# A hybrid decoder layer on one core: where the first gate/up block lies, which PSUM bank a gate product takes, and the order of the first head's query chain

## The chip, the cores and the metric

The kernel runs on one core of one Trainium2 chip. The metric is the device time of one execution in microseconds (us); the figure for a kernel is the median of its timed runs. A separate execution is taken by the hardware profiler, and every time inside the kernel below is counted from that execution's first instruction.

The engines are named as in the profile: PE (TensorE matmuls), PEld (TensorE weight loads, which overlap PE), DVE (VectorE), ACT (ScalarE), POOL (GpSimd) and SP (SyncE, which here only issues transfers). SBUF is the working memory, PSUM the memory into which PE writes, in banks of 128 x 512 float32.

## The reference, cut to what matters

One decoder layer over 16 learned meta tokens and 512 tokens, width 2048, float32:

```python
h = concatenate([meta, x])
n = rmsnorm(h, g_mix)
q, k, v, gb, gc, u = split(n @ w_in)              # 8 heads x 128, and 1024 convolution channels
q, k = rmsnorm per head(q, g_q), rmsnorm per head(k, g_k)
o_attn = stick_breaking_attention(q, k, v)        # strictly causal, log space, reverse cumulative sum
o_conv = gb * causal_dwconv3(gc * u, conv_w)
o = concatenate([rmsnorm(o_attn, g_attn_out), rmsnorm(o_conv, g_conv_out)])
h = h + o @ w_out
n2 = rmsnorm(h, g_ffn)
h = h + (silu(n2 @ w_gate) * (n2 @ w_up)) @ w_down
return h[16:]
```

A row of the attention is `w = exp(log_beta + log_pass)` with `log_pass` the sum of `log(1 - beta)` over the later keys.

## The kernel before, in words

**Arithmetic.** Everything lies transposed, channels on partitions and tokens along the free axis. A float32 value is kept as two float32r parts: `hi` (an ACT cast) and `lo` (a DVE subtraction of `hi` from the value). A product is then three matmuls, hi x hi, hi x lo and lo x hi. `split` (L349) does this for activations, `split_quad` (L196) for a piece of weights: the ACT cast is L203, the DVE subtraction L206. Three such pieces fit into `sw_split`, so the cast of a piece waits until PE has read the piece three places earlier. `prepare` (L235) makes the next piece and issues the load of a later one from SP (`load_wide`, L177, `load_quad`, L168). A piece of kind "wide" is 1024 rows of one 128-column tile.

**Stages.** First come the eight heads (`head`, L551). For head 0 the products of k, q and v run interleaved while x is loaded (L448 to L459); for head h >= 1 they run one after another (`pk`, `pq`, `pv`), and the small steps of earlier heads are threaded between their matmuls: `after(n, work)` (L316) sets work to be written down n ticks later, and `tick` counts one k tile of a product. So the k product of head 1 carries ticks 1 to 16 after head 0's own products, its q product ticks 17 to 32. The order on each engine is then made by a list scheduler, which goes by priority and by its own estimate of when each instruction is ready; `tc.high_priority` raises the priority, `tc.issue_after(i)` puts what follows behind instruction i where it is on the same engine, and `tc.keep_in_program_order` fixes the place as written. No engine changes that order at run time.

`qk_norm` (L525) gives the normalised k or q: the squares are split (`sh`, `sl`), `finish` sums them over partitions on PE (`ss_...`, L537), adds eps on DVE (L539), and calls `rsqrt` (L352), which is ACT Ln, Exp and Square (L356 to L358) and DVE steps L360, L361 and L362, the last of which writes the result; then `split` casts it (ACT L350) and makes the low part (DVE L350). `attend` (L586) turns v with PE transposes (L590) and splits it, then computes the logits `z` in three blocks of keys, b = 2, 1, 0 (L605 to L610), the log terms on ACT (L631 to L633) and DVE (L634, L635), the causal masks on POOL (L622). `sums` (L653) adds up over later keys on PE into `c` (L658 to L664), and `mix` (L688) multiplies with v. Small PSUM tiles (`small`, L66) come from the pool `sm` of four banks in rotation; `pp` holds two buffers of two banks each for products of 528 or 512 columns.

After the heads come the first convolution channels: `pc0`, `pu0` and the gate products `pb0` (L762) and `pb1` (L824), each read out by one DVE multiplication (L765, L826). Then `sm` and `pp` are released and `xyz` (two buffers each of one bank, y, z and x) takes their place.

**Strassen-like pairs.** All later products but the output projection run as pairs: `pair_product` (L875) makes seven blocks of matmuls (`block_product`, L846: L862, L865, L866) into the banks y, x and z, in place of eight. For gate/up the seven activation blocks `acts[0]` to `acts[6]` are eight tiles of 128 x 256 each, hi and lo. The first pair uses them in the order 5, 0, 1, 2, 3, 4, 6; the later ones in the order 0, 1, 2, 3, 4, 5, 6. There are 44 gate/up pairs.

**Around the output projection.** `oapool` holds `oa_last` (attention's outputs of heads 4 to 7) and `oc_hi`; `ocpool` holds the low parts of the convolution's outputs. Output tile i is the product over `oa` (all attention heads), then over `oc`. The blocks f5, f0 to f3 are made on chip, column by column, as the tiles end. The blocks f4 and f6 find no room and are written to DRAM (`fx`, L1130) column by column, from POOL. Once tile 15's products are written down (i = KT - 2), `oapool`, `ocpool` and `mpool` are released, and f4 and f6 are given places on that memory (L1067 to L1069). Then `load_f(4, 7)` (L1071) loads f4 in two transfers, hi and lo, of seven columns; the eighth is made on chip (`fifth_block`). `load_f(6, 8)` (L1133) loads f6 likewise with eight columns, after the last store to `fx`. A tile laid over released memory waits for those that used the tiles under it.

Counted from the start of the left part of `mpool`, in bytes per partition, and worked out from the shapes in the code: `mpool` 0 to 16704, `ocpool` to 33280, `oa_last` 33280 to 49664, `oc_hi` 49664 to 66048. Before the change f4 lies at 15712 to 32352 and f6 at 32352 to 48992.

Of the kernel before, what the change touches and what calls it, by code (L numbers as in the profile page):

```python
# [33 lines left out]
def hybrid_layer(ctx: ExitStack, tc: tile.TileContext, xT, w_in, w_out, w_gu, w_down, vecs, out):  # L34
# [118 lines left out]
    READ_FIRST = (*range(CONV + 9, CONV + 13), *range(CONV + FT, SIX))  # L153
    latest, opened, cast, put_off = [None], [None], [None], []

# [79 lines left out]
    def prepare():  # L235
        kind, i, s = pieces[len(split_w)]
        with tc.high_priority():
# [7 lines left out]
            if kind == "wide":  # L245
                split_quad(wide[i, s], 8)
                load_wide(i, s + 4)
                return
# [103 lines left out]
    def rsqrt(dst, v, n, y=None, t=None, eng=ve, times=None):  # L352
# [8 lines left out]
        eng.scalar_tensor_tensor(t[:, :n], t[:, :n], -0.5, v, ALU.mult, ALU.mult)  # L361
        eng.scalar_tensor_tensor(dst, t[:, :n], 1.5, y[:, :n], ALU.add, ALU.mult)  # L362
        return last

# [160 lines left out]
    def qk_norm(read, dst, parts_of, name, at=("sh", "sl")):  # L525
# [7 lines left out]
        def finish():  # L533
            v = t512(L, "v", 2)[:, :cols]
            for a, b in cuts:
# [5 lines left out]
                )  # L541
            rsqrt(dst, v, cols, times=raw)
            hi, lo, n = parts_of
            split(hi, lo, dst[:, :n])

        return finish

    selected = [None]
    SEG = [(0, 512), (512, 912), (912, 1344)]

    def head(h):  # L551

        if h:
            pk = pp.tile([P, 2, 512], F32, tag="pp", name=f"pk{h}")
            product(parts_of_all(pk), n_hl)
        read = read_qk(flat(pk), g_k, L) if h else read_k0
        kn = kns[0]
# [24 lines left out]
        else:  # L582
            after(2, scale_v)
        after(6 if h else 15, lambda: attend(h, kn, kh, kl, qn, qh, ql, vts[0]))

    def attend(h, kn, kh, kl, qn, qh, ql, vt):  # L586

# [8 lines left out]
        ve.tensor_copy(v32[:, :P], ta[:, 384:512])  # L596
        ve.tensor_copy(v32[:16, P:], tb[:16, :P])


        zs = {}  # L600
# [106 lines left out]

        after(14, lambda: sums(2))

# [51 lines left out]
    conv3(y0, cu0, 0)  # L761
    pb = pp.tile([P, 2, 512], F32, tag="pp", name="pb0")  # L762
    product([(pb[:, 0, :], META, L)], n_hl)
    gb0 = t512(L, "v", 2)[:, :SEQ]
    ve.tensor_tensor(gb0, pb[:, 0, :], r[:, META:], ALU.mult)  # L765
    assert not waiting
# [57 lines left out]
    pb = pp.tile([P, 2, 512], F32, tag="pp", name="pb1")  # L824
    product([(pb[:, 1, :], META, L)], n_hl)
    ve.tensor_tensor(gb1, pb[:, 1, :], r[:, META:], ALU.mult)  # L826
    sm.release()
# [128 lines left out]
    for j in range(1, HEADS):  # L956
        conv_pair(j, scale_a if j == 1 else None)
        if j == 1:
            gated(ocf[1], 1, ocf[1], gb1, gb1)
        elif j == 2:  # L960
            scale_a_rest()
        elif j % 2:
            gate_pair(j)
    mixp.release()
    oapool = open_pool("oapool")
# [4 lines left out]
    oa_last = oapool.tile([P, 4, 2, SEQ], F32R, name="oa_last")  # L970
    oa_at += [oa_last[:, h] for h in range(4)]
    for h in range(HEADS):
        gp.dma_start(oa_at[h], oa_dram[h])
# [24 lines left out]
    def pad(pool, n):  # L998
        pool.tile([P, n // 4], F32, name=f"pad_{pool.name}")

# [35 lines left out]
    for i, j in enumerate(OUT_TILES):  # L1036
# [6 lines left out]
        if i == KT - 2:  # L1043
# [115 lines left out]
    def h_scale_rest():  # L1159
        with tc.issue_after(opened[0].ins):  # L1160
            last = waiting_h.pop()()
        with tc.issue_after(last.ins):
            sc.preload_act_table_set("silu_and_others")
# [214 lines left out]
```

## Time and profile before

| | |
|---|---|
| timed runs | 2032.9, 2033.38 and 2033.34 us; median 2033.34 us |
| the profiled execution | 2035.46 us; its span from the first to the last instruction 2033.8 us |
| mean granted TensorE clock | 0.999 of full speed |
| PE busy | 2023.1 us, 99% of the span |
| DVE busy | 1725.6 us, 85% |
| ACT busy | 1078.3 us, 53% |

The profile page gives the busy time of each engine, the span in 40 slices and the costliest groups of instructions. The view of the waits lists for one engine what it waited for. The timeline gives the instructions of an engine in order: start, duration, engine, line, operation, output and inputs, shape, and in brackets the idle time before it with what released it. The windows give for a stretch of time the busy time of each engine, the granted PE clock, the share of the DMA engines in use and their rate. A matmul's recorded duration overlaps with the next one's, since they are pipelined: a matmul of 512 columns starts about 0.23 us after the one before it, one of 256 columns about 0.11 us.

### The profile page before, as it was taken

The page shows a single profiled execution, that of the slowest core. Times are in us where ns is not written, and L with a number is a line of the kernel's source. Part 1 is how long each engine was busy: PE and PEld are TensorE (multiplying, and loading weights), DVE is VectorE, ACT ScalarE, POOL GpSimd, SP SyncE. Part 2 cuts the span into 40 slices and gives each one's busy share as a digit, 9 for nine tenths or more (in the row PEclk, how much of TensorE's full clock was granted, in tenths as well). Part 3 has the DMA queues.
Part 4 walks back from the last instruction along what each step waited for, and adds up shares of the span by engine and source line. Part 5 has one row for each costly group of instructions (what it writes and reads, how often), then busy time and mean ns, then how long its engine had stood idle before and what let it go on. Part 6 is the DMA issues. An engine that isn't in the chain of part 4 may idle for free.

```text
span 2033.8 us, 39697 instructions
## 1 busy us (share of the span) xinstructions
PE 2023.1 (99%) x16158; PEld 1963.8 (97%) x16158; DVE 1725.6 (85%) x2199; ACT 1078.3 (53%) x1559; POOL 339.4 (17%) x507
## 2 busy tenths in 40 slices
PE   9999999999999999999999999999999999999999
PEld 9899999899998889999999999999999999999999
DVE  7777777698887878999998988988988978888888
ACT  7776666444454444555555555555555554444443
POOL 0111111200014440112111111111111243131211
PEclk9999999999999999999999999999999999999999
DMA  6243344833365555557555555555555999797864
GB/s 221 94 146 125 116 144 127 281 104 106 103 207 171 171 160 193 151 151 208 150 166 162 143 175 161 143 174 161 145 172 161 278 342 350 171 315 200 222 146 93
DMA packets 156664, 356.31 MB, mean 175 GB/s; under 512 B 13696, under 2 KB 68224, under 8 KB 155712
## 3 DMA queue, kind: packets, MB, share of 16 engines
q1 hardware_dynamic: 72784, 216.76, 33.7%
q0 software_dynamic: 83696, 136.99, 25.4%
q8 instruction: 127, 2.08, 0.4%
q14 instruction: 57, 0.47, 0.1%
HBM read 275.78 MB, written 77.92 MB: 174 GB/s over the span
## 4 chain that ended last, share of the span: by engine, by line
PE 96%; DVE 1%; ACT 1%; DMA 1%; issue 0%; POOL 0%; SPq 0%; ACTq 0%; POOLq 0%; DVEq 0%
PE x L862 13%; PE x L865 13%; PE x L866 13%; PE z L862 7%; PE z L865 7%; PE z L866 7%; PE y L862 3%; PE y L865 3%; PE y L866 3%; PE pv L339 3%; PE pk L339 3%; PE pq L339 2%; PE pv L337 1%; PE pk L337 1%; PE pq L337 1%; DMA f<-fx 1%
## 5 line engine op out<-in xcount | busy, mean ns | idle before, releaser
L203 ACT CAST sw_split<-sw_in 128x1024 fp32r<-128x1024 f32 (+3 forms) x671 | 662.5, 989 | 707.3 <-PE x L865 173.4
L206 DVE TENSOR_TENSOR sw_split<-sw_in,sw_split 128x1024 fp32r<-128x1024 f32 (+3 forms) x671 | 776.7, 1158 | 145.4 <-ACT sw_split L203 137.9
L865 PE MATMUL x<-f,sw_split 128*128 128x256 f32 x1408 | 388.1, 276 | 2.2 <-DMA f<-fx 2.2
L862 PE MATMUL x<-f,sw_split 128*128 128x256 f32 x1408 | 388.2, 276 | 0.2 <-ACT sides L887 0.2
L866 PE MATMUL x<-f,sw_split 128*128 128x256 f32 x1408 | 387.9, 276 | 0.0
L865 PEld LDWEIGHTS x<-f,sw_split 128*128 128x128 f32 x1408 | 265.1, 188 | 2.4 <-DMA f<-fx 2.4
L862 PEld LDWEIGHTS x<-f,sw_split 128*128 128x128 f32 x1408 | 265.0, 188 | 1.1 <-ACT sides L887 0.6
L866 PEld LDWEIGHTS x<-f,sw_split 128*128 128x128 f32 x1408 | 265.0, 188 | 0.0
L1179 POOL DMA_DIRECT2D fd<-s x147 | 103.7, 922 | 711.0 <-DVE s L350 635.4
L862 PE MATMUL z<-f,sw_split 128*128 128x256 f32 x704 | 193.6, 275 | 0.0
L865 PE MATMUL z<-f,sw_split 128*128 128x256 f32 x704 | 193.6, 275 | 0.0
L866 PE MATMUL z<-f,sw_split 128*128 128x256 f32 x704 | 193.6, 275 | 0.0
L216 DVE TENSOR_TENSOR sw_in<-sw_in 128x1024 f32<-128x1024 f32 (+1 forms) x164 | 187.7, 1145 | 6.1 <-DMA sw_in<-w_in 1.2
L862 PE MATMUL x<-ring,sw_split 128*128 128x256 f32 x608 | 167.2, 275 | 0.0
L865 PE MATMUL x<-ring,sw_split 128*128 128x256 f32 x608 | 167.2, 275 | 0.0
L866 PE MATMUL x<-ring,sw_split 128*128 128x256 f32 x608 | 167.2, 275 | 0.0
L862 PEld LDWEIGHTS z<-f,sw_split 128*128 128x128 f32 x704 | 132.2, 188 | 0.0
L865 PEld LDWEIGHTS z<-f,sw_split 128*128 128x128 f32 x704 | 132.2, 188 | 0.0
L866 PEld LDWEIGHTS z<-f,sw_split 128*128 128x128 f32 x704 | 132.1, 188 | 0.0
L862 PEld LDWEIGHTS x<-ring,sw_split 128*128 128x128 f32 x608 | 114.1, 188 | 0.0
L866 PEld LDWEIGHTS x<-ring,sw_split 128*128 128x128 f32 x608 | 114.1, 188 | 0.0
L865 PEld LDWEIGHTS x<-ring,sw_split 128*128 128x128 f32 x608 | 114.1, 188 | 0.0
(698 smaller groups left out, 5280.7 us busy)
## 6 DMA issues: line engine op xcount, KB each, us to landing
sw_in<-w_gu SPq DMA_DIRECT2D x176, 512.0 KB, 4.1
sw_in<-w_in SPq DMA_DIRECT2D x90, 512.0 KB, 3.5
fd<-s POOLq DMA_DIRECT2D x147, 256.0 KB, 5.2
sw_in<-w_down SPq DMA_DIRECT2D x96, 384.0 KB, 4.3
ring<-fd POOLq DMA_DIRECT2D x42, 768.0 KB, 17.6
sw_in<-w_out SPq DMA_DIRECT2D x32, 512.0 KB, 3.5
out_T<-d POOLq DMA_DIRECT2D x54, 256.0 KB, 4.8
mix_dram<-st_x POOLq DMA_DIRECT2D x16, 516.0 KB, 4.1
```

The lines of the kernel that those rows point to most:

```text
L203: cast[0] = sc.copy(hi, src)
L206: latest[0] = ve.tensor_tensor(lo, src, hi.bitcast(F32), ALU.subtract)
L216: return ve.tensor_tensor(sums[name], a, b, ALU.add)
L337: pe.matmul(ps, wh, ah[:, a:b], start=k + i == 0, stop=False)
L339: pe.matmul(ps, w, x[:, a:b], start=False, stop=k + i == last and x is (al if used[0] <= n_first else ah))
L862: opening = pe.matmul(p, hi[:, kk], ah, start=start and j == k == 0, stop=False, skip_group_check=skip)
L865: pe.matmul(p, hi[:, kk], al, start=False, stop=False, skip_group_check=skip)
L866: pe.matmul(p, lo[:, kk], ah, start=False, stop=k == n - 1, skip_group_check=skip)
L1179: gp.dma_start(fd[c][s][:, :, k], t[:, :, i])
```

## The change

It has three parts.

1. **f4 and f6 change places.** f6 is laid first, at 15712 to 32352; a pad of 1024 bytes follows, and f4 goes to 33376 to 49776, without the 60 spare elements at its end (`slots` has a parameter for them). A pad of 128 bytes behind `oa_last` moves `oc_hi` to 49792. So f4 now lies over `oa_last` and that pad alone, and f6 over `ocpool` and the end of `mpool`. The order in which they are loaded stays: f4, then f6.
2. **`pb0` goes to a small bank** (the pool `sm`) in place of a buffer of `pp`. The next tile, `pb1`, so takes the other of `pp`'s two buffers, and its first bank in place of the second.
3. **The first head's query chain.** The split of head 0's k (cast and subtraction) is put off until the Square (L358) of its q chain has been issued on ACT. The DVE low part of a "wide" piece of weights, the second one prepared after that, is issued behind the DVE low part of q. Head 1's reads of its k product (L435, L436) are issued behind the ACT cast of head 0's q. The turning of v (`turned`) stays at tick 15, and the logits are written down at tick 21 in place of 15; `sums(2)` follows 9 ticks later in place of 14, at tick 30 in place of 29. `rsqrt` returns its last instruction too, for the bookkeeping.

```diff
-    latest, opened, cast, put_off = [None], [None], [None], []
+    latest, opened, cast, put_off, behind = [None], [None], [None], [], []
...
             if kind == "wide":
-                split_quad(wide[i, s], 8)
+                low = split_quad(wide[i, s], 8, later=True)
+                first = behind.pop(0) if behind else None
+                with tc.issue_after(first.ins) if first else nullcontext():
+                    low()
                 load_wide(i, s + 4)
...
-            rsqrt(dst, v, cols, times=raw)
+            last, _ = rsqrt(dst, v, cols, times=raw)
             hi, lo, n = parts_of
-            split(hi, lo, dst[:, :n])
+            if name == "k0":
+                split_k0.append(lambda: split(hi, lo, dst[:, :n]))
+                return
+            if name != "q0":
+                split(hi, lo, dst[:, :n])
+                return
+            with tc.issue_after(last.ins):
+                split_k0.pop()()
+            split_q0.extend(split(hi, lo, dst[:, :n]))
+            behind.extend([None, split_q0[1]])
...
-        read = read_qk(flat(pk), g_k, L) if h else read_k0
+        with tc.issue_after(split_q0[0].ins) if h == 1 else nullcontext():
+            read = read_qk(flat(pk), g_k, L) if h else read_k0
...
-        after(6 if h else 15, lambda: attend(h, kn, kh, kl, qn, qh, ql, vts[0]))
-
-    def attend(h, kn, kh, kl, qn, qh, ql, vt):
+        if h:
+            after(6, lambda: attend(h, kn, kh, kl, qn, qh, ql, turned(h, vts[0])))
+        else:
+            after(15, lambda: vts.append(turned(h, vts[0])))
+            after(21, lambda: attend(h, kn, kh, kl, qn, qh, ql, vts[1]))
+
+    def turned(h, vt):
...
-        after(14, lambda: sums(2))
+        after(14 if h else 9, lambda: sums(2))
...
-    pb = pp.tile([P, 2, 512], F32, tag="pp", name="pb0")
-    product([(pb[:, 0, :], META, L)], n_hl)
+    pb = small("pb0")
+    product([(pb, META, L)], n_hl)
...
-    product([(pb[:, 1, :], META, L)], n_hl)
-    ve.tensor_tensor(gb1, pb[:, 1, :], r[:, META:], ALU.mult)
+    product([(pb[:, 0, :], META, L)], n_hl)
+    ve.tensor_tensor(gb1, pb[:, 0, :], r[:, META:], ALU.mult)
...
+    pad(oapool, 128)
...
-    def slots(pool, dt, m, n, name, **kw):
+    def slots(pool, dt, m, n, name, tail=60, **kw):
...
-        t = pool.tile([P, c + 64], dt, name=name, **kw)
+        t = pool.tile([P, 4 + c + tail], dt, name=name, **kw)
...
-            for s in (4, 6):
-                acts[s] = slot(fpool_last, F32R, 8, f"f{s}", f"f{s}")
+            acts[6] = slot(fpool_last, F32R, 8, "f6", "f6")
+            pad(fpool_last, 1024)
+            acts[4] = slots(fpool_last, F32R, 1, 8, "f4", tail=0)[0]
```

More of the change, by code (lines that the diff above doesn't have):

```diff
@@ L361, in rsqrt @@
         eng.scalar_tensor_tensor(t[:, :n], t[:, :n], -0.5, v, ALU.mult, ALU.mult)
-        eng.scalar_tensor_tensor(dst, t[:, :n], 1.5, y[:, :n], ALU.add, ALU.mult)
-        return last
+        return last, eng.scalar_tensor_tensor(dst, t[:, :n], 1.5, y[:, :n], ALU.add, ALU.mult)
     def square_sum(acc, src, first, s=None, eng=gp):
@@ L541, in finish @@
                 )
-            rsqrt(dst, v, cols, times=raw)
+            last, _ = rsqrt(dst, v, cols, times=raw)
             hi, lo, n = parts_of
-            split(hi, lo, dst[:, :n])
+            if name == "k0":
[8 more added lines that the diff above has]
+            behind.extend([None, split_q0[1]])
         return finish
+    split_k0, split_q0 = [], []
     selected = [None]
@@ L597, in attend @@
         ve.tensor_copy(v32[:16, P:], tb[:16, :P])
+        return vh, vl, v32
+    def attend(h, kn, kh, kl, qn, qh, ql, v):
+        vh, vl, v32 = v
         zs = {}
@@ L761, in hybrid_layer @@
     conv3(y0, cu0, 0)
-    pb = pp.tile([P, 2, 512], F32, tag="pp", name="pb0")
-    product([(pb[:, 0, :], META, L)], n_hl)
+    pb = small("pb0")
+    product([(pb, META, L)], n_hl)
     gb0 = t512(L, "v", 2)[:, :SEQ]
-    ve.tensor_tensor(gb0, pb[:, 0, :], r[:, META:], ALU.mult)
+    ve.tensor_tensor(gb0, pb, r[:, META:], ALU.mult)
     assert not waiting
@@ L963, in hybrid_layer, with pad @@
             gate_pair(j)
+    def pad(pool, n):
+        pool.tile([P, n // 4], F32, name=f"pad_{pool.name}")
     mixp.release()
@@ L996, in slot @@
         return slots(pool, dt, 1, n, name, tag=tag)[0]
-    def pad(pool, n):
-        pool.tile([P, n // 4], F32, name=f"pad_{pool.name}")
     acts = {}
@@ L1160, in h_scale_rest @@
         with tc.issue_after(opened[0].ins):
-            last = waiting_h.pop()()
+            last, _ = waiting_h.pop()()
         with tc.issue_after(last.ins):
```

## The prediction, made before the changed kernel was run

> **What bounds the kernel now.** The page first, then the view of PE's waits.
>
> ```profile
> span 2033.8 us, 39697 instructions
> ...
> PE 2023.1 (99%) x16158; PEld 1963.8 (97%) x16158; DVE 1725.6 (85%) x2199; ACT 1078.3 (53%) x1559; POOL 339.4 (17%) x507
> ```
>
> ```profile
> PE x L865 <- DMA f<-fx: 2.2, 1, 2.2
> PE warm L84 <- DVE one L80: 1.1, 1, 1.1
> ```
>
> PE is the bound, and the change takes away no matmul. What it can win is PE's idle time: the span less the busy time is 10.7 us, and the longest wait is for f, the second is the kernel's start. Only four waits stand where the change acts: this one, and those of z, y and c, whose rows follow below with their idle time in brackets.
>
> The f wait costs more than its 2.2 us. The windows for PE alone set the undisturbed block before it against the block that waits, both of 24 matmuls; the last number but two is the granted clock:
>
> ```profile
> 781.22:783.94 2.72, 2.72 (x26) 1.00 1.08 414
> 784.61:791.45 6.84, 4.67 (x24) 0.75 0.30 102
> ```
>
> ```profile
> 784.62 0.38 PE L862 MATMUL x<-f,sw_split 128*128 128x256 f32 x1
> 787.16 0.58 PE L865 MATMUL x<-f,sw_split 128*128 128x256 f32 x1 [2.16 <-DMA f<-fx]
> ```
>
> 6.84 - 2.72 = 4.12 us: the second matmul comes 2.54 us after the first in place of 0.11, which is 2.43, and the other 1.7 follow it. The windows of all engines tell why:
>
> ```profile
> 788.00:789.00 1.00, 1.00 (x6) 1.00 (x6) 0.98 (x1) 0.00 (x0) 0.00 (x0) 0.50 0.70 250
> ```
>
> Ahead of the DMA share stands the clock: it is halved, and the mean of 0.75 over 6.84 us makes that half clock 3.4 us long. Half of it, 1.7 us, is lost.
>
> **Part 1, f4 and f6.** The block is the seventh of the first pair, the one that reads f6; f4 had landed. The timeline of POOL shows the issues:
>
> ```profile
> 757.23 0.71 POOL L1130 DMA_DIRECT2D fx<-w  x1 [0.92 <-DVE w L350]
> ...
> 761.69 1.29 POOL L371 TENSOR_TENSOR acc_h<-acc_h,sw_in 128x512 f32<-128x512 f32 x1 [0.61 <-ACT sw_in L370]
> 763.90 0.70 POOL L1130 DMA_DIRECT2D fx<-w  x1 [0.92 <-DVE w L350]
> 767.91 2.87 POOL L1019 DMA_DIRECT2D f<-fx  x4 [3.32 <-PE po15z L842]
> ```
>
> ```profile
> DMA to landing us min/median/max: 7.9/11.4/17.1
> ```
>
> ```profile
> fx<-w POOLq DMA_DIRECT2D x15, 256.0 KB, 2.7
> ```
>
> All four loads of f (the view of that tile on POOL has their times to landing) go out from 767.91, 0.72 us apart (2.87 / 4), released by the last product over the convolution's outputs. The last, issued at about 770.0, lands 17.1 us later, at 787.1, which is when PE goes on. The rates say what it waits for:
>
> ```profile
> 760.00:765.00 5.00, 5.00 (x36) 4.69 (x35) 4.26 (x6) 3.16 (x6) 2.77 (x4) 1.00 0.14 52
> 765.00:770.00 5.00, 5.00 (x44) 5.00 (x43) 3.88 (x8) 2.29 (x5) 2.09 (x3) 1.00 0.67 174
> 770.00:775.00 5.00, 5.00 (x47) 5.00 (x46) 4.46 (x7) 3.77 (x8) 0.78 (x2) 1.00 1.03 327
> ```
>
> From 770 the DMA engines are full; before 765 they idle at a share of 0.14. After the change f4 waits for attention's outputs alone, and PE is done with those here:
>
> ```profile
> 761.59 0.39 PE L842 MATMUL po15x<-oa_last,sw_split 128*128 128x512 f32 x1
> 761.81 0.28 PE L840 MATMUL po15y<-oc_hi,sw_split 128*128 128x256 f32 x1
> ...
> 767.56 0.28 PE L862 MATMUL y<-f,sw_split 128*128 128x256 f32 x1
> ```
>
> So f4's place is free at 762.0 and not at 767.7. Its seventh column was stored at 757.23, and a store lands in 2.7 us (the median of the 15 stores to `fx` above), so that is no limit. POOL is in L371 until 763.0; I put the issue there, 4.9 us earlier. f6 still waits for 767.7 and for its own last column, stored at 763.90. f4's two issues of 0.72 us now stand in POOL's queue ahead of that store or behind it, so it is late by 0 to 1.4 us; nobody but f6 waits for it. Were f4's issue put ahead of L371, POOL would stand for 0.3 us until 762.0, with that sum and the store behind it. SP's loads of weights meet f4's traffic from 763 to 770; at shares of 0.14 and 0.67 there is room, and a piece that landed late would hold PE for as much.
>
> f4's two transfers carry 1.8 MB (128 partitions x 7 x 256 x 4 bytes, twice) and f6's 2.1 MB, worked out from the code. The last of the four landed at 787.1; with f4's share begun 4.9 us earlier on idle engines f6 lands at 787.1 - 4.9 = 782.2. The other bound is a store that queues behind all of f4: the median of 11.4 us parts f4's landings from f6's, so f4 would land by 763.0 + 11.4 = 774.4; then come the store, 2.7, and f6's own stretch, 787.1 - (767.9 + 11.4) = 7.8: 784.9. It is needed at 784.7. I take no wait: 4.1 us won, and the half clock with it. By 0.3 at most the wait is given back: without it the next pair comes 4.1 us earlier upon DVE, whose queue is not paced by PE there:
>
> ```profile
> 791.92 1.05 ACT L203 CAST sw_split<-sw_in 128x1024 fp32r<-128x1024 f32 x1
> ```
>
> ```profile
> 789.28 1.23 DVE L275 TENSOR_TENSOR sw_in<-sw_in 128x1024 f32<-128x1024 f32 x1
> 790.43 1.22 DVE L216 TENSOR_TENSOR sw_in<-sw_in 128x1024 f32<-128x1024 f32 x1
> ```
>
> The third block of that pair would begin at 784.62 + 3 x 2.72 = 792.8. Its weights are what L275 makes; they are cast after it, from 790.5 in 1.05 us, and the low part is a DVE step as large as L216's, 1.22 us from 791.65: 792.9. That is at the limit, so I count 0.2. **Part 1: -3.9 us**, between 0 (f6 as late as now) and -4.1.
>
> **Part 2, the small bank.** The wait view names an ACT cast for y; the timelines of PE and DVE show another releaser, 0.15 us ahead:
>
> ```profile
> 388.30 0.61 PE L339 MATMUL pb<-n,sw_split 128*128 128x512 f32 x2
> 389.79 0.36 PE L862 MATMUL y<-n,sw_split 128*128 128x258 f32 x1 [0.87 <-ACT sw_split L203]
> ```
>
> ```profile
> 388.95 0.69 DVE L826 TENSOR_TENSOR gb<-pb,r 128x512 f32<-128x512 f32 x1 [3.35 <-PE pb L339]
> ```
>
> DVE reads `pb1` out until 389.64, while y's weights may be cast as soon as `pb0`'s are used, before `pb1` begins. y's bank lies on that buffer of `pp`: the pool hands out its two buffers in turn, and by the count of allocations `pb1` is in the first one, on which the first bank of `xyz` falls. With `pb0` gone from `pp`, `pb1` is in the second, below z. z comes two blocks after y, some 5.4 us, when L826 is long over. The last matmul starts at 388.52, y could at 388.75: **1.0 us won**, between 0 (if it were the cast) and 1.04. `pb0`'s new bank served head 7's logits, which are read before that head's sums, and it is read out a whole product (16 k tiles of three matmuls, 16 x 0.68 = 10.9 us) before x takes that bank: nothing; a reader still at work would cost up to its 0.69 us.
>
> **Part 3, the query chain.** Timelines of ACT, DVE and PE:
>
> ```profile
> 55.17 0.51 ACT L350 CAST host<-kn 128x384 fp32r<-128x384 f32 x1 [0.95 <-DVE kn L362]
> 55.59 0.63 ACT L358 ACTIVATE tmp<-tmp 128x512 f32<-128x512 f32 x1
> ...
> 59.44 0.62 ACT L350 CAST host<-tmp 128x512 fp32r<-128x512 f32 x1 [0.28 <-DVE tmp L362]
> ```
>
> ```profile
> 57.59 1.20 DVE L206 TENSOR_TENSOR sw_split<-sw_in,sw_split 128x1024 fp32r<-128x1024 f32 x1
> 58.73 0.67 DVE L362 SCALAR_TENSOR_TENSOR tmp<-tmp,tmp 128x512 f32<-128x512 f32 x1
> ```
>
> ```profile
> 58.67 0.39 PE L337 MATMUL pq<-n,sw_split 128*128 128x512 f32 x1
> 60.11 0.80 PE L605 MATMUL z<-host,host 128*128 128x272 f32 x3 [1.05 <-ACT host L350]
> ```
>
> The first logits wait for the cast of q (59.44 to 60.06), and that chain is held up twice: its Square stands on ACT behind the cast of k, idle for 0.95 us first, and a weight piece's low part of 1.20 us stands on DVE ahead of its last step. Both go. Then the Square starts 0.95 us sooner or more, L362 by another 1.1, and the cast of q ends by about 58.1 (it may meet a weight cast on ACT). PE reaches z at 58.67 + 0.23 = 58.9; tick 21 is five k tiles, 15 matmuls, into the q product, and z stood behind the 16th: the same place. So 60.11 - 58.9 = **1.2 us won**, between 0 and 1.2. What moves behind I cost at nothing: the key casts are needed at the same z; head 1's two reads of `pk` come later by one cast, 0.62 us, and feed head 1's logits, which come after its v product; the weight piece is for that v product, more than ten k tiles of q (7 us) away, and behind it waits one SP load, of a piece four places on, with loads after it that wait for later pieces anyway. Without that cover the piece would cost up to its 1.20 us.
>
> Then the sums over later keys:
>
> ```profile
> 68.31 0.39 PE L339 MATMUL pq<-n,sw_split 128*128 128x512 f32 x1
> 69.20 0.43 PE L658 MATMUL c<-sph,later_r 128*128 128x432 f32 x1 [0.50 <-ACT lw L633]
> ```
>
> 0.66 us lost. The whole chain shifts with z, but PE also arrives 1.2 us sooner; only the later tick (0.68 us at most) and the moved weight step help. Between 0 and 0.66, I take **0.3**.
>
> **The sum** is 3.9 + 1.0 + 1.2 + 0.3 = 6.4 us. The profiled execution took 2035.46 us (span 2033.8); 2035.46 - 6.4 = 2029.1, or 0.31% less. The median, 2.1 us below the profiled one, becomes 2033.34 - 6.4 = **2026.9 us**.
>
> The Trainium skill speaks of the halved clock ("TensorE: Matmul & The Clock Gate", "What's actually happening"): the clock halves after at least one idle window of some 3.4 us, which runs freely. The half-clock stretch agrees in length; the idle time, 2.2 us, is shorter than the page's window. By the free-running window the loss would depend on the phase of an execution, which is the first rival.
>
> **Rivals.**
>
> - *The half clock isn't in the timed runs.* The three differ by 0.5 us, and the profiled one is 2.1 us longer, which leaves room for 1.7. Then part 1 is worth 2.4 - 0.2 and the time is 2028.6. For: that difference. Against: nothing ties it to this place. 0.13.
> - *f6 stays the late one, or f4 isn't issued earlier.* The store of f6's last column would land behind all of f4, or POOL would keep f4's issue behind it. For: the last landing may be tight, 784.9 against 784.7. Against: the idle DMA engines. In full, part 1 is 0 and the time 2030.8; with half the wait and no half clock about 2028.5. 0.16, three quarters of it near 2030.8.
> - *Another wait at head 0.* The scheduler orders all engines anew, and the logits or sums find some other step late: 1.5 us less, 2028.4. 0.07.
> - *f4's new place reads slowly*, the rival on the other side. The 48 matmuls of 256 columns from 761.81 to 767.56 take 0.120 us each on `oc_hi`, the 24 on f 2.72 / 24 = 0.113. Read at 0.120, f4's 44 x 24 matmuls cost 1056 x 0.0067 = 7.1 us, more than the 6.4 won: 2034.0; f6, which moves too, as much again: 2041.1. It decides from 6 ns a matmul on. Against: that block of 2.72 us reads f4 at its old place; f6 moves to just that place, by 16640 bytes, f4 by 17664, both multiples of 256. 0.06, half of it for each size.
>
> The forecast keeps 0.53; 0.05 is for an order elsewhere that I can't see. **Chances.** A measurement of this kernel can tell some 0.2%, 4.1 us, from no change, so faster means below 2029.3: 0.53 and 0.13, 0.04 of the second rival and 0.06 of the third, 0.76. Slower: 0.03 of the slow place and 0.03 of the unseen, 0.06. Same: 0.18. The forecast's own range is 2026.1 to 2028. The wide one reaches from 2025.9 (all four waits gone, 7.0, and a crumb) to 2030.8 (part 1 worth nothing).
>
> **What would show it.** Right: f4's issues near 763 and no wait for f in PE's waits; a granted clock of 1.00 from 780 to 795; y directly after `pb1`; z directly after `pq`, with the Square ahead of the key cast. Wrong: L1019 still at 768, or f6 landing past 785; a y that waits for another bank; a new wait at c; f blocks that take more than 2.72 us in every pair.

## The result, and the profile after

The median of 16 runs fell from 2033.12 to 2029.41 us: a ratio of 0.9981, 95% interval 0.9973 to 0.9989. That is 3.7 us where 6.4 were forecast. The time lies in the prediction's wide range (2025.9 to 2030.8) and outside its own narrow one (2026.1 to 2028), 2.5 us above the forecast. The fall is just short of the 4.1 us that the prediction had set as its bound for "faster", to which it gave 0.76; to no change it gave 0.18.

The two profiled executions differ by more: 2035.46 and 2029.19 us, 6.3 us apart, nearly the forecast's sum. Most of this document is about why these two differences are not the same.

The page of the changed kernel, and its view of PE's waits:

```profile
span 2027.5 us, 39699 instructions
...
PE 2020.7 (100%) x16158; PEld 1961.9 (97%) x16158; DVE 1725.5 (85%) x2199; ACT 1078.1 (53%) x1559; POOL 336.6 (17%) x507
```

```profile
PE warm L84 <- DVE one L80: 1.1, 1, 1.1
PE pk L340 <- ACT n L412: 1.0, 2, 0.7
PE z L627 <- DVE host L353: 0.3, 1, 0.3
PE x L883 <- ACT sides L908: 0.2, 1, 0.2
```

The waits for f, y and c are gone; that of z has shrunk from 1.1 to 0.3 and changed its releaser. The wait of pk, at the kernel's start, differs between traces from nothing to 1.8 us and isn't part of the change. (In the changed kernel L337 has become L340, L339 L342, L350 L353, L357 L360, L358 L361, L362 L365, L605 L626, L862 L883, L865 L886, L1019 L1041.)

**f.** POOL's timeline, and the last line of the view of `f` on POOL:

```profile
759.30 1.29 POOL L373 TENSOR_TENSOR acc_h<-acc_h,sw_in 128x512 f32<-128x512 f32 x1 [0.71 <-ACT sw_in L372]
761.51 0.70 POOL L1153 DMA_DIRECT2D fx<-w  x1 [0.92 <-DVE w L353]
762.10 1.56 POOL L1041 DMA_DIRECT2D f<-fx  x2
766.42 1.42 POOL L1041 DMA_DIRECT2D f<-fx  x2 [2.75 <-DMA fx<-w]
```

```profile
DMA to landing us min/median/max: 6.3/9.7/12.1
```

f4 is issued at 762.1, behind the last store, and f6 at 766.4 and 767.1, once that store has landed. The last one lands at the latest 767.1 + 12.1 = 779.2 us, and PE wants it at 782.5. (PE's timeline runs 2.3 us earlier here than in the profile of before: this block began at 784.62 there and begins at 782.28 now.) The windows around that place:

```profile
774.00:782.20 8.20, 8.20 (x71) 7.79 (x69) 7.67 (x14) 4.16 (x7) 0.00 (x0) 1.00 0.93 343
782.25:785.00 2.75, 2.72 (x23) 2.72 (x24) 2.25 (x2) 0.39 (x1) 0.00 (x0) 1.00 0.01 3
```

In this stretch PE is busy for 2.72 of 2.75 us, the clock is 1.00, and the DMA engines have nothing left to do (share 0.01). By the starts of its matmuls the block that waited takes 2.88 us, since its first one takes 0.23 in place of 0.11, with a wait or without. So what it lost in the profile of before is 6.83 - 2.88 = 4.0 us and not the 4.1 that the prediction had from the block ahead of it.

**y** starts right behind `pb1`, and **c** right behind `pq` (PE's timeline):

```profile
386.14 0.62 PE L342 MATMUL pb<-n,sw_split 128*128 128x512 f32 x2
386.60 0.28 PE L883 MATMUL y<-n,sw_split 128*128 128x258 f32 x1
```

```profile
68.08 0.61 PE L342 MATMUL pq<-n,sw_split 128*128 128x512 f32 x2
68.53 0.36 PE L679 MATMUL c<-sph,later_r 128*128 128x432 f32 x1
```

**z** still loses time. PE and ACT:

```profile
58.34 0.61 PE L342 MATMUL pq<-n,sw_split 128*128 128x512 f32 x2
59.09 0.39 PE L626 MATMUL z<-host,host 128*128 128x272 f32 x1
59.82 0.39 PE L627 MATMUL z<-host,host 128*128 128x272 f32 x1 [0.33 <-DVE host L353]
```

```profile
55.35 0.63 ACT L361 ACTIVATE tmp<-tmp 128x512 f32<-128x512 f32 x1 [1.01 <-DVE kn L365]
55.89 0.50 ACT L353 CAST host<-kn 128x384 fp32r<-128x384 f32 x1
...
58.42 0.62 ACT L353 CAST host<-tmp 128x512 fp32r<-128x512 f32 x1 [0.70 <-DVE tmp L365]
```

z could start 2 x 0.227 after 58.34, at 58.79, and comes 0.30 later; its second matmul comes 0.73 after the first in place of 0.13, another 0.60. The Square (L361) now stands ahead of the key cast, but it still idles 1.01 us for the last step of k.

To split the whole difference I took each matmul's start less that of the one before it, less the usual value for its size, from the two traces. The f block gives 4.0 us, y 1.04, the stretch of head 0 from 50 to 100 us 2.24 (z 0.3, c 0.7, and 1.2 in small gaps, most of them at the matmuls of the sums), and an x block of the convolution at 428 us, 0.39. That makes 7.7. The output projection takes back 1.4: its matmuls start 229 ns apart in place of 227. What is left, 6.3, agrees with the two spans.

### The profile page after: what moved, and what is told of

The parts are those of the page before. It is cut to its first block, busy times and chain, and to the rows that moved or that the text cites. A ratio compares the mean times of both kernels' runs of the same rounds, so it can differ in the third digit from the quotient of the medians.

```text
span 2027.5 us, 39699 instructions
## 1 busy us (share of the span) xinstructions
PE 2020.7 (100%) x16158; PEld 1961.9 (97%) x16158; DVE 1725.5 (85%) x2199; ACT 1078.1 (53%) x1559; POOL 336.6 (17%) x507
## 4 chain that ended last, share of the span: by engine, by line
PE 95%; DVE 2%; ACT 1%; issue 1%; DMA 1%; SPq 0%; POOL 0%; ACTq 0%; DVEq 0%
PE x L883 13%; PE x L886 13%; PE x L887 13%; PE z L886 7%; PE z L883 7%; PE z L887 7%; PE y L886 3%; PE y L887 3%; PE y L883 3%; PE pv L342 3%; PE pk L342 3%; PE pq L342 3%; PE pv L340 2%; PE pk L340 1%; PE pq L340 1%; PE pb L342 1%
## 5 line engine op out<-in xcount | busy, mean ns | idle before, releaser
L883 PE MATMUL x<-f,sw_split 128*128 128x256 f32 x1408 | 387.6, 275 | 0.3 <-ACT sides L908 0.2
L886 PE MATMUL x<-f,sw_split 128*128 128x256 f32 x1408 | 387.3, 275 | 0.0
L883 PEld LDWEIGHTS x<-f,sw_split 128*128 128x128 f32 x1408 | 264.3, 188 | 1.1 <-ACT sides L908 0.6
L886 PEld LDWEIGHTS x<-f,sw_split 128*128 128x128 f32 x1408 | 264.3, 188 | 0.0
L883 PE MATMUL z<-f,sw_split 128*128 128x256 f32 x704 | 193.6, 275 | 0.0
L886 PE MATMUL z<-f,sw_split 128*128 128x256 f32 x704 | 193.6, 275 | 0.0
L883 PE MATMUL x<-ring,sw_split 128*128 128x256 f32 x608 | 167.2, 275 | 0.0
L886 PE MATMUL x<-ring,sw_split 128*128 128x256 f32 x608 | 167.2, 275 | 0.0
L886 PEld LDWEIGHTS z<-f,sw_split 128*128 128x128 f32 x704 | 132.1, 188 | 0.0
L883 PEld LDWEIGHTS z<-f,sw_split 128*128 128x128 f32 x704 | 132.1, 188 | 0.0
L883 PEld LDWEIGHTS x<-ring,sw_split 128*128 128x128 f32 x608 | 114.1, 188 | 0.0
L886 PEld LDWEIGHTS x<-ring,sw_split 128*128 128x128 f32 x608 | 114.1, 188 | 0.0
```

Of the source, the lines that this page charges most:

```text
L883: opening = pe.matmul(p, hi[:, kk], ah, start=start and j == k == 0, stop=False, skip_group_check=skip)
L886: pe.matmul(p, hi[:, kk], al, start=False, stop=False, skip_group_check=skip)
```

## The experiments

Each experiment was timed beside the kernel before on the same chip. "Lowest" is the lowest run of each; where a landing varies it tells more than the median.

| kernel | median, us (runs) | lowest | before beside it: median, lowest | ratio and 95% interval |
|---|---|---|---|---|
| before again | 2031.84 (11) | 2031.48 | 2032.01, 2031.15 | 0.9999 (0.9990 to 1.0007) |
| part 1 alone | 2032.86 (11) | 2032.46 | 2032.01, 2031.15 | 1.0002 (0.9993 to 1.0011) |
| parts 2 and 3 | 2028.36 (11) | 2027.38 | 2032.01, 2031.15 | 0.9983 (0.9975 to 0.9992) |
| changed, pad of 256 | 2027.75 (11) | 2027.23 | 2032.01, 2031.15 | 0.9977 (0.9968 to 0.9986) |
| the same, Square freed | 2026.90 (7) | 2026.70 | 2032.18, 2031.31 | 0.9972 (0.9961 to 0.9983) |
| part 2 alone | 2031.11 (11) | 2030.51 | 2032.18, 2031.31 | 0.9995 (0.9986 to 1.0004) |
| ticks alone | 2032.16 (11) | 2031.23 | 2032.18, 2031.31 | 1.0002 (0.9994 to 1.0011) |
| part 1 alone, pad of 256 | 2031.60 (11) | 2031.28 | 2032.67, 2031.56 | 0.9992 (0.9983 to 1.0001) |
| part 3 alone | 2029.62 (11) | 2028.65 | 2032.67, 2031.56 | 0.9986 (0.9977 to 0.9995) |
| order alone | 2030.36 (11) | 2029.13 | 2032.67, 2031.56 | 0.9986 (0.9977 to 0.9995) |
| Square freed alone | 2029.65 (11) | 2029.05 | 2032.67, 2031.56 | 0.9986 (0.9977 to 0.9995) |

Medians of different rows come from different sittings; they are compared through the column of before.

### The kernel before, once more

No edit.

> The kernel before, unchanged, to see its executions one by one. Two theories of the 2 us by which its profiled execution (2035.46 us) lies above its median (2033.1), and of why the medians part by 3.7 us where the two profiled executions part by 6.3. Varying landing: when f6 lands differs from execution to execution, and with it the wait for f (2.2 us) and the half clock (1.7 us); then the spans scatter over some 4 us, the long ones have a mean clock of 0.999 and the short ones 1.000, and a profile of a short execution shows no wait or a small one for f. Fixed wait: the wait for f stands in every execution, and the scatter comes from elsewhere (the start, the end, work on PE throughout); then clock and span are not tied, and another profile shows the same 4.1 us at this block.

Varying landing, plainly. This profile has no wait for f at all; its three longest waits are

```profile
PE warm L84 <- DVE one L80: 1.1, 1, 1.1
PE z L605 <- ACT host L350: 1.1, 1, 1.1
PE y L862 <- ACT sw_split L203: 0.9, 1, 0.9
```

and f's landing line, which had a median of 11.4 and a maximum of 17.1, reads

```profile
DMA to landing us min/median/max: 5.7/9.1/14.1
```

Over 100 runs of this kernel (33, 23 and 33 beside the other experiments, and these 11), the median is 2032.1 us. In 15 the mean granted clock is 0.999, and these take 2034.82 us or more; in the other 85 it is 1.000, and none takes over 2034.26. 31 of the 100 lie above 2033. The profile that the prediction was made from, 2035.46 us at a clock of 0.999, is such a one.

The windows of both kernels show what is late. Of the profiled execution of before, the last 1.8 us before f6 lands; of this one, the last 1.4:

```profile
784.90:785.90 1.00, 0.11 (x1) 0.00 (x0) 1.00 (x2) 0.00 (x0) 0.00 (x0) 1.00 0.16 61
785.90:786.70 0.80, 0.00 (x0) 0.00 (x0) 0.80 (x1) 0.00 (x0) 0.00 (x0) 1.00 0.11 41
```

```profile
783.40:783.80 0.40, 0.40 (x6) 0.40 (x5) 0.40 (x2) 0.00 (x0) 0.00 (x0) 1.00 1.02 410
783.90:784.90 1.00, 0.95 (x7) 0.51 (x6) 0.69 (x3) 0.00 (x0) 0.00 (x0) 1.00 0.84 332
```

In the late one a share of 0.11 to 0.16 of the 16 engines works, about two of them, while PE stands idle; in the other the transfer ends with all at work. The late execution's last 12 packets of f end one every 0.16 to 0.33 us from 783.2 to 786.6, while in this one the last 12 end within 1.05 us. So f6 isn't late because its traffic is too much; by the share, one or two DMA engines still have a tail to move when the others are done. Why they fall behind is open.

### Part 1 alone, and the output projection

```diff
+    pad(oapool, 128)
...
-            for s in (4, 6):
-                acts[s] = slot(fpool_last, F32R, 8, f"f{s}", f"f{s}")
+            acts[6] = slot(fpool_last, F32R, 8, "f6", "f6")
+            pad(fpool_last, 1024)
+            acts[4] = slots(fpool_last, F32R, 1, 8, "f4", tail=0)[0]
```

> Part 1 alone on the kernel before: the places of f4 and f6 and the pads, PE's order unchanged. By the prediction -3.9 us against a profiled execution that has the full wait and the half clock. By the theory that the landing varies and that the 128-byte pad under oc_hi costs 1.3 us in the output projection: the wait for f gone in the profile, the matmuls on oc_hi and oa at 230 ns in place of 227, and the median of the timed runs only 1 to 2.5 us below before. If the pad has no part in the slower output projection, those matmuls stay at 227 ns here.

The part that the prediction valued at 3.9 us gives nothing in the median, and the 1 to 2.5 us expected here didn't come either: the median is 0.85 us above that of before. Its lowest run is 1.3 us above the lowest of before, and its highest, 2033.38, is 2.2 us below the highest of before, 2035.57. It narrows the runs to 0.9 us and puts them all higher. The windows of 100 us in the output projection, of before again, part 1 alone, the changed kernel and the changed kernel with a pad of 256 bytes, count PE's matmuls in the bracket behind its busy time:

```profile
610.00:710.00 100.00, 100.00 (x443) 82.84 (x442) 77.74 (x103) 43.84 (x74) 42.93 (x49) 1.00 0.57 174
```

```profile
610.00:710.00 100.00, 100.00 (x439) 82.10 (x438) 76.94 (x101) 43.11 (x74) 42.58 (x48) 1.00 0.56 171
```

```profile
610.00:710.00 100.00, 100.00 (x439) 82.07 (x438) 77.74 (x100) 42.72 (x73) 41.60 (x48) 1.00 0.57 172
```

```profile
610.00:710.00 100.00, 100.00 (x442) 82.79 (x442) 78.74 (x102) 43.17 (x73) 41.67 (x48) 1.00 0.56 174
```

All four are 100% busy. Where `oc_hi` lies 128 bytes from its old place, 439 fit in place of 442 or 443: PE is slower, and no wait shows it. By the start times the slow ones are the products on `oc_hi` and the first on `oa` behind them, most of them 228 to 234 ns in place of 227.

### The pad at 256 bytes, and at 64

```diff
-    pad(oapool, 128)
+    pad(oapool, 256)
```

> The changed kernel with a pad of 256 bytes behind oa_last in place of 128, so that oc_hi lies a multiple of 256 bytes from its old place (49920 in place of 49792); every engine's order is the same. If the place of oc_hi modulo 256 slows the output projection: matmuls on it back at 227 ns, 1.3 us less, a median of 2028.1. If the rate hangs on something else (f4's and f6's loads, the places of other tiles, chance): 230 ns stays, and the median is within 0.5 us of 2029.4.

It is the place of `oc_hi`: 227 ns again, and a median of 2027.75. The sum of all gaps behind matmuls of 512 columns is 299.80 us here and 301.17 in the changed kernel, 1.37 apart. And on the kernel before, where f4 and f6 stay where they were:

```diff
     oa_at += [oa_last[:, h] for h in range(4)]
+    oapool.tile([P, 16], F32, name="pad_oa")
```

> One look at the kernel before with a pad of 64 bytes behind oa_last: only oc_hi moves, to 64 bytes past a multiple of 256. If any place off a multiple of 256 is slow, the matmuls on oc_hi take about 231 ns in place of 227 as with the 128-byte pad; if only an offset of 128 is slow, 227. Either shows by the same stroke that the pad does it without the new places of f4 and f6.

```profile
610.00:710.00 100.00, 100.00 (x435) 81.47 (x434) 76.08 (x98) 42.41 (x71) 42.00 (x47) 1.00 0.55 169
```

435 in place of 443, 1.8% fewer, so some 4 ns more for each. 64 bytes cost more than 128, and the new places of f4 and f6 have no part in it. The single run took 2035.23 us, with a wait for f of 0.3. That 64 bytes cost more than 128 rests on one trace of each.

### Parts 2 and 3 without part 1

```diff
+            for s in (4, 6):
+                acts[s] = slot(fpool_last, F32R, 8, f"f{s}", f"f{s}")
-            acts[6] = slot(fpool_last, F32R, 8, "f6", "f6")
-            pad(fpool_last, 1024)
-            acts[4] = slots(fpool_last, F32R, 1, 8, "f4", tail=0)[0]
...
-    pad(oapool, 128)
```

> Parts 2 and 3 without part 1: f4 and f6 at their old places, no pads. The two traces give 1.0 us for y's bank, 0.7 us for the sums and 0.3 us for the logits, 2.0 us together, so a median of about 2031.1; the prediction has 2.5, 2030.6. The output projection's matmuls on oc_hi stay at 227 ns if the pad is what slows them, and go to 230 if it is something in parts 2 or 3. The wait for f comes back, of a size that varies if the landing does. A rival: parts 2 and 3 interact with part 1, since all engines are ordered anew, and this one is no better than before.

The fall is 3.7 us where 2.0 were expected: the small gaps around the sums (1.2) and the x block (0.4) weren't in that sum. Without part 1 the median is 1.1 us below that of the changed kernel. The lowest run, 2027.38, is that of the changed kernel with the 256-byte pad (2027.23), but the highest is 2031.73 against 2028.14. Part 1 is worth the spread: 4.4 us against 0.9. It doesn't take away every late run, though: one of the 16 runs of the changed kernel itself, 2031.56 us, has a mean clock of 0.999, the only one of them below 1.000. It left no trace, so what it waited for isn't known. The profiled execution is one with a wait (what the clock does behind it stands in the last section):

```profile
783.48 0.39 PE L886 MATMUL x<-f,sw_split 128*128 128x256 f32 x1 [2.26 <-DMA f<-fx]
```

### Part 1 alone with the pad of 256 bytes

```diff
-    pad(oapool, 128)
+    pad(oapool, 256)
```

(on part 1 alone)

> Part 1 alone on the kernel before, with the 256-byte pad, so without the slow reads of oc_hi. Theory: part 1 only takes away the late landings of f6 that some executions have; then no run waits for f and none has the half clock, the runs lie within 1 us of each other, and the median is 0 to 0.6 us below before (2031.5 to 2032.1). Rival: the prediction's 3.9 us, a median of about 2028.3, would show if the wait stood in every execution. A third: the new places slow f's own blocks; then the median is above before.

The highest of 11 runs is 2032.75 us where before has 2035.71, no run has a clock below 1.000, the lowest is that of before within 0.3, and the median is 1.1 us below a median of before that was itself high in this sitting (2032.67, against 2032.01 and 2032.18 in the other two). The runs spread over 1.5 us where 1 was expected. That is part 1's worth: some 0.3 us by the lowest runs and 1.1 by the medians, by how many executions of before land late, and 3 to 4 in the tail. The interval of the ratio reaches 1.0001, so for the median alone even this is not shown.

### Part 2 alone

```diff
-    pb = pp.tile([P, 2, 512], F32, tag="pp", name="pb0")
-    product([(pb[:, 0, :], META, L)], n_hl)
+    pb = small("pb0")
+    product([(pb, META, L)], n_hl)
...
-    product([(pb[:, 1, :], META, L)], n_hl)
+    product([(pb[:, 0, :], META, L)], n_hl)
```

> Part 2 alone on the kernel before. Theory of the prediction: y waited for DVE's read of pb1, because both lie on one bank, so the wait of 1.04 us at 389 goes and nothing else changes: a median 1.0 us below before. Rival: y waited for the ACT cast that the view of the waits names; then the wait stays and the time with it. A second look at the x block at 428, which lost 0.39 us before and not after: if that went with the banks of xyz it is gone here too, 1.4 us in all; if with part 3 or the order of the engines it stays.

1.1 us in the medians, 0.8 in the lowest; the wait of y is gone, and the x block at 428 us keeps its 0.39. The time alone doesn't show it (the interval of the ratio includes 1), the trace does: y now starts at 388.86 us, while the ACT cast that the view of the waits named runs from 388.83 to 389.89 and DVE's read of `pb1` from 389.06. So the cast was not the releaser; DVE's read, with `pb1` in y's bank, fits as argued.

### The query chain: ticks, order, and a buffer

Part 3 alone:

```diff
+            with tc.issue_after(last.ins):
+                split_k0.pop()()
...
+            after(21, lambda: attend(h, kn, kh, kl, qn, qh, ql, vts[1]))
...
+        after(14 if h else 9, lambda: sums(2))
```

> Part 3 alone on the kernel before: order and ticks. The traces give 0.3 us at the logits, 0.7 at the first sums, 0.9 in small gaps at the matmuls of the sums and 0.4 at the x block of 428 us (which stayed with part 2 alone): 2.3 us, a median of about 2029.8. The prediction has 1.5 us, 2030.6. If the parts only work together, within 0.5 us of before.

The median is as expected, and the lowest run is 2.9 us below that of before. The trace gives the 2.24 and 0.39 of the changed kernel. Its ticks without its order, on the kernel before:

```diff
-        after(6 if h else 15, lambda: attend(h, kn, kh, kl, qn, qh, ql, vts[0]))
...
+            after(15, lambda: vts.append(turned(h, vts[0])))
+            after(21, lambda: attend(h, kn, kh, kl, qn, qh, ql, vts[1]))
...
-        after(14, lambda: sums(2))
+        after(14 if h else 9, lambda: sums(2))
```

> Of part 3 only the ticks, on the kernel before: v is turned at tick 15, the logits are written down at 21 and the sums at 30; the order of the casts, of the Square and of the weight piece is left to the scheduler as before. Theory: the sums gain by their later tick (0.67 us of wait and some 0.9 us of small gaps at the matmuls of the sums go), the logits need the order of ACT and DVE (their loss of 1.2 us stays), so a median 1.5 us below before. Rival: the ticks do nothing by themselves, since PE's place of the logits is the same and the sums hang on the logits' chain: within 0.4 us of before.

Nothing: my theory of the sums fell. z waits as before, and so do the sums (0.39 and 0.47 late). The order without the ticks (the edit is against part 3 alone):

```diff
...
-            after(21, lambda: attend(h, kn, kh, kl, qn, qh, ql, vts[1]))
+        after(6 if h else 15, lambda: attend(h, kn, kh, kl, qn, qh, ql, turned(h, vts[0])))
...
-        after(14 if h else 9, lambda: sums(2))
+        after(14, lambda: sums(2))
```

> Part 3 without its ticks: the key casts behind the Square, the weight piece's low part behind q's, head 1's reads behind q's cast, and the logits and sums written down at ticks 15 and 29 as before. The ticks alone gave nothing. Theory: the order does it all, and the time is that of part 3 whole within 0.3 us. Rival: the order only pays with the later ticks, since with the earlier ones the scheduler places the logits' matmuls one by one among q's and the sums meet the same chain: 1 us or more above part 3 whole.

The sums are on time, the logits aren't:

```profile
59.17 0.81 PE L622 MATMUL z<-host,host 128*128 128x272 f32 x3 [1.05 <-DVE v L609]
```

(L622 is L605 of before; the copy of v that the row names ends at 59.13, the cast of q at 59.12.) The wait is 1.05 us as before the change, and the median is 0.7 us above part 3 whole, between the 0.3 of the theory and the 1 of the rival. So the order pays for the sums, and the ticks only with it, for a part of z.

Then the Square's own wait. By the code, `rsqrt` takes two tiles from a rotation of three: k's chain has two, q's chain has the third and, for the Square's output, k's first, which the last step of k (L365) reads. The Square can't start before that step ends, wherever it stands in ACT's queue. With q's tile of squares, which is free by then, in its place:

```diff
-            last, _ = rsqrt(dst, v, cols, times=raw)
+            last, _ = rsqrt(dst, v, cols, times=raw, t=s if name == "q0" else None)
```

> The changed kernel with the 256-byte pad and one edit more: the Square of head 0's q writes into the tile of squares that q no longer needs, in place of the next of three buffers in rotation, which is the one that the last step of k's chain (L365) still reads. Theory: this buffer is why the Square did not move (it still waits 1.0 us for L365 of kn on ACT), and behind it the cast of q, its low part and the logits are late. Then the Square starts about 1.0 us sooner, the logits lose nothing in place of 0.9 us, and the median is 0.9 us below the 2027.75 us of the 256-byte pad alone: 2026.9. Rival: DVE is the limit there (three steps of k and three of q in a row, with a low part and two copies of v between); then the Square comes sooner, the logits still lose 0.5 us or more, and the median is within 0.4 us of 2027.75.

2026.90, as the theory had it; by the starts of the matmuls the stretch from 50 to 100 us loses 0.9 us less than with the pad alone. The Square follows the Exp at once, and PE's waits are down to the start and 0.2 us:

```profile
53.58 0.63 ACT L360 ACTIVATE tmp<-tmp 128x512 f32<-128x512 f32 x1
54.24 0.63 ACT L361 ACTIVATE tmp<-tmp 128x512 f32<-128x512 f32 x1
55.16 0.51 ACT L353 CAST host<-kn 128x384 fp32r<-128x384 f32 x1 [0.28 <-DVE kn L365]
```

```profile
PE warm L84 <- DVE one L80: 1.1, 1, 1.1
PE x L883 <- ACT sides L908: 0.2, 1, 0.2
```

This is the best version: 5.3 us below before. The same line of code alone, on the kernel before:

```diff
-            rsqrt(dst, v, cols, times=raw)
+            rsqrt(dst, v, cols, times=raw, t=s if name == "q0" else None)
```

> None of the change: the kernel before with only the Square of head 0's q writing into q's tile of squares instead of the third buffer in rotation. Theory: this false dependence is the largest part of the logits' loss; ACT's Square starts about 1.0 us sooner, and if the scheduler then puts the weight piece's low part behind q's last step by itself, the 1.2 us of z go: about 1.2 us below before, and with the sums' gaps up to 2.2. Rival: the weight piece of 1.2 us on DVE still stands ahead of q's last step, so z gains 0.3 us or less and the change's order is needed too.

2029.65 us: by the median as much as all of part 3 (2029.62), by the lowest runs and the traces the gain is 0.4 us smaller. The rival was right for z, which gains 0.2 and still loses 0.59 at the cast of q and 0.45 at its low part, the latter because the weight piece stands ahead of that on DVE:

```profile
57.31 1.21 DVE L206 TENSOR_TENSOR sw_split<-sw_in,sw_split 128x1024 fp32r<-128x1024 f32 x1
58.45 0.68 DVE L350 TENSOR_TENSOR host<-tmp,host 128x512 fp32r<-128x512 f32 x1
```

The gain is in what follows the logits: the waits and small gaps of the sums are gone, and the x block's 0.39 at 428 us with them. Why that block gains was not followed.

## Why the prediction was right or wrong

- **The f wait as a bound.** The row was read rightly and taken for more than it is. 2.43 us of wait and 1.7 of half clock are what *that* execution lost; in the traced one of 2031.67 us neither is there, and of 100 runs 85 have no half clock and 69 take 2033 us or less. The 6.4 us were taken from the median of 2033.34, and a median like that holds little of part 1's 3.9. The prediction had the hint, a profiled execution 2.1 us above the median, and gave the rival built on it (the half clock isn't in the timed runs) 0.13, with the wait left in. The wait belonged to that rival too.
- **Part 1's mechanism** was right: f4's issue within the 0 to 1.4 us behind 763 that were allowed for (762.1, which is 764.4 on the timeline of before), f6 behind the store (which took 3.7 us to land where 2.7 were reckoned), the last landing at 779.2 (781.5) at the latest where 782.2 was reckoned, no wait and a clock of 1 in the profile. The 0.2 us on DVE were not given back. The size, 3.9, holds between two profiled executions (4.0) and is 0.3 to 1.1 for the median.
- **Part 2** was right in releaser, bank and size: 1.0 forecast, 1.04 in the trace.
- **Part 3, z**: "Both go" is the step that failed. The weight piece went; the Square's idle 0.95 us was put down to the cast of k that stands ahead of it in the queue, and was a buffer in rotation. The row could not tell the two apart: the cast ahead of the Square waited for the same instruction (kn L362), so the Square would have been late behind it or by itself. z gave 0.3, not 1.2; freeing the buffer gave the rest.
- **Part 3, the sums**: 0.3 forecast. c's whole 0.66 went, with 1.2 us in gaps of 0.1 to 0.2, most at the other matmuls of the sums and too small to have a row in the waits, and 0.39 at the x block of 428 us. That the later tick would help the sums is refuted by the ticks alone, which gave nothing; the order, or the freed buffer by itself, did it.
- **The pad of 128 bytes was not priced.** It was in the diff and in the list of places, and its 1.4 us are a term that the sum lacks. The rival of slow reads had the right mechanism, with its price per matmul, and looked at f4, whose blocks take 2.72 us as ever, and not at `oc_hi`, though it leaned on moves by multiples of 256 and `oc_hi` moved by 128.
- **The sum.** For an execution without a late landing: 1.0 + 2.2 + 0.4 - 1.4 = 2.2 us, from about 2031.7 (the lower runs beside the changed kernel) to 2029.5. The other 1.4 of the 3.7 is that 11 of those 16 runs of before lie above 2032.2, 6 of them above 2034, which lifts their median to 2033.12. That late landings do this is shown for the long runs by the clock; for those between, one trace has it (the ticks alone, profiled at 2033.84 us, with a wait for f of 1.3 and no half clock). That 2029.41 lies in the wide range is so in part luck: the range's upper end stood for a part 1 worth nothing, which was near the truth. That the two profiled executions agree with 6.4 is chance: part 1's 4.0 was there in the one, and the query chain's surplus (2.6 in place of 1.5) met the pad's 1.4.
- **A sum in the rivals.** "Half the wait and no half clock" comes out at 2026.9 + 1.2 = 2028.1 us and not about 2028.5. And of the 48 matmuls at 0.120 us that the rival of slow reads takes for reads of `oc_hi`, one in three reads `oc_lo`. Neither moves the forecast.

## What to carry to other kernels

A wait for a transfer in one profile is one draw: before pricing it, set the profiled time against the timed runs, and if it stands above them, price the wait as a share of the executions. An engine that idles may wait for a buffer in rotation rather than for its place in the queue; count the tiles that the chain takes before moving its instructions. And a pad can change the rate at which PE reads a tile: PE at 100% busy can lose time, and the number of matmuls in a window tells.

## What the runs showed of the hardware that was not expected

**The granted clock is decided window by window.** Between the kernel's start and its end the record of the clock in the traces changes at steps of 3.413 us only: before's full-speed stretches of 781.652 and 1242.451 us are 229 and 364 of them, that of parts 2 and 3 alone, 2024.104, is 593. Where the steps fall differs between executions: the first full-speed stretch begins 4.0 to 7.1 us after the first instruction. Windows laid on that grid, for before, part 3 alone and parts 2 and 3 (the PE busy time, the clock, the DMA share and rate):

```profile
783.63:787.05 3.42, 1.33 (x8) 1.00 0.40 156
787.05:790.46 3.41, 3.30 (x15) 0.50 0.48 156
```

```profile
781.08:784.49 3.41, 1.70 (x11) 1.00 0.32 126
784.49:787.91 3.42, 3.42 (x19) 0.50 0.46 153
```

```profile
779.25:782.66 3.41, 1.92 (x13) 1.00 0.53 211
782.66:786.08 3.42, 2.60 (x22) 1.00 0.49 158
```

Of these, a window in which PE is busy for 1.33 or 1.70 us is followed by one at half clock; one with 1.92 is not. But the recorded busy time isn't the measure: at the kernel's end, in the run with the 64-byte pad and in part 1 alone, less was enough for full speed in the window behind.

```profile
2028.13:2031.55 3.42, 1.56 (x14) 1.00 0.34 120
2031.55:2034.96 3.41, 0.00 (x0) 1.00 0.10 33
```

```profile
2025.96:2029.38 3.42, 1.60 (x15) 1.00 0.33 117
2029.38:2032.79 3.41, 0.00 (x0) 1.00 0.11 36
```

Counted by the columns of the matmuls that start in a window (1792, 2560 and 3072 in the three above, 3072 in each of these two), all 14 traces agree: 2560 or fewer are followed by half clock, 2688 or more by full clock. The wait in the third kernel, 2.26 us, is longer than that in the second, 1.7, but falls across two windows. So a wait of some 2 us costs 1.7 us more or nothing, by where it falls. The Trainium skill ("TensorE: Matmul & The Clock Gate", "What's actually happening") has a free-running window of 3413 ns, which these runs show; its "≥1 idle window" is stricter than they are, since a window partly idle was enough.

**The rate of PE hangs on where `oc_hi` lies.** At its old place and 256 bytes from it the 512-column products run at 227 ns; 128 bytes from it the window above holds 439 of them in place of 443, 64 bytes from it 435. The products on `oa`, which did not move, are slow too where they follow those on `oc_hi`. f6 and f4 begin 16 bytes into their places, at 15728 and 33392, which is 112 bytes past a multiple of 256 from `oc_hi`'s old place, and both are read at 0.113 us per 256 columns. So it isn't a rule of one distance for every tile; what collides there was not tried.
